# Feed-forward input by block products: four double groups instead of three, two of them with sums made by accumulating transfers

## The chip, the cores and the metric

One core of one Trainium2 chip runs the whole kernel. The metric is the device time of one execution in microseconds (us); smaller is better. Each measurement is a median over several runs.

## The reference

One layer of a hybrid decoder on 256 tokens of width 1024, in float32. Only the last part matters here, the gated feed-forward block with a hidden width of 2816:

```python
hn = rmsnorm(h, norm_ffn_g[l])
gu = hn @ w_ffn_in[l]                       # (256, 1024) @ (1024, 5632)
h = h + (jax.nn.silu(gu[..., :FFN_HIDDEN]) * gu[..., FFN_HIDDEN:]) @ w_ffn_out[l]
...
return rmsnorm(h, final_norm_g)
```

Before it come the attention, the recurrent branch, the merge and the cross-attention, which the change does not touch.

## The kernel before

**Precision.** Every float32 operand of a matmul is split into a high and a low part. ScalarE (ACT) copies the operand into a rounded type (`hi`), VectorE (DVE) subtracts to get `lo`, and TensorE (PE) multiplies three times: hi by hi, hi by lo, lo by hi. For a weight tile of 128x2048 this is `halve` (lines 1098 and 1099): one ACT copy and one DVE subtraction per tile.

**Groups and units.** The hidden width is cut into 11 groups of 256. A group has an input part in two units `("I", j, kh)`, one for each half of the 1024 features, and an output unit `("O", j)`. A unit is one weight tile of 1 MB. A direct input unit does 24 matmuls of 512 columns: two token halves, four feature blocks, three products. An output unit has 24 too, and adds into four accumulators (`acc`) that live to the end.

**Seven products for eight.** A double group (two neighbouring groups, q and q + 1) has four weight blocks: two feature halves by two groups. With two token halves that is a 2x2 by 2x2 product of blocks. Done directly it takes four units, 96 matmuls. `ffn_product` does it in Strassen's way with seven block products P1, P2, P6, P7, P5, P3, P4 of 12 matmuls, 84 in all. The price is sums and differences of blocks before the products (`block` and `load_blocks`, through `both`, line 1106: two DVE instructions of 1024 columns for each sum), sums of tokens made once (`token_sums`), and sums of results (`keep` on ACT and `whole` on DVE, line 1280, tile `fc`). Each product also needs a halving of its weight block, so a double group needs seven halvings where four units need four.

**Gate and transposes.** `gate` (lines 1205 and 1208) applies the silu on ACT (`fg`) and multiplies on DVE (`fu`). When both token halves of a group are gated, `turn_hid` transposes the result on PE (`hidT`, line 1215) and `split` makes its two parts (`hids`, lines 310 and 311). The output unit of that group reads them.

**Order.** PE's order is written out by hand: `FFN_PLAN` lists the units, `TURNS` says ahead of which unit a group's transposes come, and `LOADS` ahead of which unit the four blocks of a double group are loaded. The orders of ACT, DVE, GpSimd (POOL) and of the DMA issues on SyncE (SP) are set by a planner when the kernel is built: it takes an instruction when its inputs and buffers are free by its own estimates, earlier program text first. On the chip each queue then runs in that fixed order. Before, the units are: groups 0 and 1 direct, the double group 2 and 3, group 4 direct, double group 5 and 6, group 7 direct, double group 8 and 9, group 10 direct, with output units in between.

**Buffers.** Halved tiles rotate through four places (three pairs `hi`/`lo` and one pair `px` for every fourth unit), so halving runs at most four units ahead of PE. Raw tiles for direct and output units have two buffers. The four blocks of a double group have one buffer each (`b` in the profile, tags B10, B11, B12, B6), so the next double group's loads wait until the last reads of the present one. Four banks of the accumulation memory (`mm`) serve the products A, B and F and the transposes.

**The block before the first unit.** The norm of the second token half goes through a small power on POOL (`r`, line 1164), then a scaling on ACT (`hn`), PE transposes (`h2T`) and DVE, before the second direct matmuls and the token sums.

Of the kernel before, what the change touches and what calls it, by code (L numbers as in the profile page):

```python
# [97 lines left out]
def lay(ws):  # L98
# [45 lines left out]
def build(tc, A, out):  # L144
    nc = tc.nc
    V, SC, G, PE, SY = nc.vector, nc.scalar, nc.gpsimd, nc.tensor, nc.sync
    with ExitStack() as ctx:
# [940 lines left out]
        def halve(raw, n):  # L1088
            if n % 4 == 3:
                hi, lo = px[:, 0:2048], px[:, 2048:4096]  # L1090
            else:
                hi = wh.tile([128, 2048], F32R, name="hi", tag="hi")
                lo = wl.tile([128, 2048], F32R, name="lo", tag="lo")
            pieces = 2 if n < 2 else 1
            w = 2048 // pieces
            for c in range(pieces):
                a = slice(c * w, (c + 1) * w)
                SC.activation(hi[:, a], raw[:, a], AF.Copy)  # L1098
                V.tensor_tensor(lo[:, a], raw[:, a], hi[:, a].bitcast(F32), op=ALU.subtract)  # L1099
            return hi, lo  # L1100

# [5 lines left out]

        def load_blocks(q):
            blk.clear()
            for key, tag, c in (("22", "B12", (q + 1, 1)), ("12", "B6", (q + 1, 0)),  # L1110
                                ("11", "B10", (q, 0)), ("21", "B11", (q, 1))):
                blk[key] = big(tag, "b" + key, (128, 2048))
                SY.dma_start(blk[key], A["w"][where[("I",) + c]])
# [5 lines left out]
        def less(out, x, c):  # L1119
            SC.activation(out, x, AF.Copy, scale=-1.0)  # L1120
            G.dma_start(out, A["w"][where[("I",) + c]], accum_op=ALU.add)

        def block(q, name):
            if name == "P7" and BY_DMA:
                less(blk["21"], blk["11"], (q, 1))
# [73 lines left out]
        X2 = (h2h, h2l)  # L1199
        hid, acc, psi, hm = {}, {}, {}, {}  # L1200

        def gate(o, t):
            ps = psi.pop((o, t))
            g = t2b("fg", (128, 256))
            SC.activation(g, ps[:, 0:256], AF.Silu)
            if o not in hm:
                hm[o] = t2("fu", (128, 2, 256))
            V.tensor_tensor(hm[o][:, t], ps[:, 256:512], g, op=ALU.mult)

        def turn_hid(o):  # L1210
            bk = mm.tile([128, 2, 256], F32, name="hidT", tag="mm")
# [29 lines left out]
        def token_sums():  # L1241
            a11, a12, a21, a22 = (h2g[t, c] for t in range(2) for c in range(2))

            def put(i, g):
                SC.activation(SS[:, 0, i], g, AF.Copy)
                V.tensor_tensor(SS[:, 1, i], g, SS[:, 0, i].bitcast(F32), op=ALU.subtract)

            V.tensor_tensor(a22, a21, a22, op=ALU.add)
            s2 = t2("s2", (128, 4, 128))
            V.tensor_tensor(s2, a22, a11, op=ALU.subtract)  # L1250
# [4 lines left out]
            V.tensor_tensor(a12, a12, s2, op=ALU.subtract)  # L1255
            put(3, a12)

        def tokens(name):
# [18 lines left out]

        def whole(q, t, ps, key):
            c = t2("fc")
            V.tensor_tensor(c, ps, kept.pop(key), op=ALU.add)  # L1280
            psi[q, t] = c
            gate(q, t)

        def ffn_product(n):
# [8 lines left out]
            if name == "P1":  # L1293
                keep("1", ps, t2("f1"))
            elif name == "P2":
                whole(q, 0, ps, "1")
            elif name == "P6":
                keep("2", ps, gf[:, 1024:1536])
            elif name == "P5":
                keep("4", ps, gf[:, 1536:2048])  # L1300
                whole(q + 1, 1, bank_of["F"], "4")
            elif name == "P3":
                psi[q + 1, 0] = ps
                gate(q + 1, 0)
            elif name == "P4":
                whole(q, 1, ps, "2")
# [149 lines left out]
```

## Time and profile before

| | |
|---|---|
| median of three runs | 620.22 us (620.06 to 620.54) |
| the profiled execution's own time | 619.96 us |
| its span | 618.2 us |
| PE busy | 607.5 us, 98% |
| DVE busy | 460.0 us, 74% |
| ACT busy | 355.2 us, 57% |
| POOL busy | 256.5 us, 41% |
| DMA, share of 16 engines | 46.5% for the main queue, 107.50 MB |

Times in the rows are microseconds from the start of the span, unless ns is written. PE is the matrix engine, PEld its loading of weights, which overlaps. A row such as `lo<-raw,hi` names the tile written and the tiles read; L1099 is line 1099 of the kernel. The wait lists name the engine and instruction that waited, the one it waited for, the total, the number of times and the longest. The chain of waits is followed back from the last instruction, at each step to what released it. SPq rows are issues of transfers; their length is the time to issue. The feed-forward stage runs from about 430 us to 610 us of the span.

### The profile page before, as it was taken

The numbers are of one execution on the slowest core, as the hardware profiler recorded it, in microseconds if no ns is written. First come the engines' busy times: TensorE is split into PE (matmuls) and PEld (weight loads), VectorE is DVE, ScalarE is ACT, GpSimd is POOL, SyncE is SP. The second block draws the span as 40 slices with busy tenths as digits, with TensorE's granted clock in tenths as the row PEclk, the third lists the DMA queues.
The fourth block names the chain that finished last, engine by engine and source line by source line (L and its number), as shares of the span: only waits on it lengthen the run. The fifth ranks groups of instructions, "written<-read, shape, count | busy, mean of one in ns | idle before, by whom it ended". The sixth has DMA issues, their size and how long they took to land.

```text
span 618.2 us, 8376 instructions
## 1 busy us (share of the span) xinstructions
PE 607.5 (98%) x3117; PEld 506.7 (82%) x3117; DVE 460.0 (74%) x714; ACT 355.2 (57%) x545; POOL 256.5 (41%) x227
## 2 busy tenths in 40 slices
PE   8999999999999999999999999999998999999995
PEld 7888888888877877778888888888886888888884
DVE  7589988979766875747855456655799897997743
ACT  7785554334376756736456566746567556565432
POOL 3888744556544464355876876720000000000003
PEclk9999999999999999999999999999999999999999
DMA  8753553334543333644454554463815718613311
GB/s 346 289 204 150 205 200 140 137 136 140 189 150 136 137 137 124 208 181 149 191 205 152 193 200 156 163 227 142 335 68 193 283 69 325 218 68 137 141 64 68
DMA packets 16888, 107.50 MB, mean 174 GB/s; under 512 B 2000, under 2 KB 2640, under 8 KB 4560
## 3 DMA queue, kind: packets, MB, share of 16 engines
q1 hardware_dynamic: 16128, 106.14, 46.5%
q10 hardware_dynamic: 720, 0.84, 0.4%
q8 instruction: 24, 0.39, 0.2%
q14 instruction: 16, 0.13, 0.1%
HBM read 105.92 MB, written 1.05 MB: 173 GB/s over the span
## 4 chain that ended last, share of the span: by engine, by line
PE 89%; DVE 7%; issue 1%; ACT 1%; DMA 1%; POOL 0%; POOLq 0%; DVEq 0%; ACTq 0%
PE pst L263 13%; PE pst L265 13%; PE pst L264 13%; PE psf L284 7%; PE pqA L1269 4%; PE psf L285 4%; PE acc L265 3%; PE acc L263 3%; PE acc L264 3%; DVE lo L1099 2%; PE psi L263 2%; PE psi L265 2%; PE pqF L1269 2%; PE psi L264 2%; PE lp L638 2%; DVE b L1106 1%
## 5 line engine op out<-in xcount | busy, mean ns | idle before, releaser
L223 POOL TENSOR_TENSOR lo<-raw,hi 128x448 fp32r<-128x448 f32 x106 | 161.7, 1540 | 110.6 <-ACT hi L219 107.8
L219 ACT ACTIVATE hi<-raw 128x1024 fp32r<-128x1024 f32 (+1 forms) x128 | 128.7, 1028 | 93.7 <-PE pst L265 58.1
L223 DVE TENSOR_TENSOR lo<-raw,hi 128x576 fp32r<-128x576 f32 (+2 forms) x128 | 131.1, 1031 | 57.2 <-ACT hi L219 54.2
L263 PE MATMUL pst<-hi,XX 128*128 128x512 f32 x224 | 90.5, 404 | 0.0
L265 PE MATMUL pst<-hi,XX 128*128 128x512 f32 x224 | 87.4, 390 | 0.0
L264 PE MATMUL pst<-lo,XX 128*128 128x512 f32 x224 | 87.4, 390 | 0.0
L1374 POOL TENSOR_TENSOR hg<-H,gf 128x512 f32<-128x512 f32 x3 | 3.8, 1290 | 172.1 <-DVE H L1366 172.1
L1099 DVE TENSOR_TENSOR lo<-raw,hi 128x2048 fp32r<-128x2048 f32 (+1 forms) x21 | 43.7, 2086 | 12.2 <-ACT hi L1098 12.1
L265 PEld LDWEIGHTS pst<-hi,XX 128*128 128x128 f32 x224 | 42.1, 188 | 9.0
L263 PEld LDWEIGHTS pst<-hi,XX 128*128 128x128 f32 x224 | 42.1, 188 | 8.8 <-issue 0.7
L264 PEld LDWEIGHTS pst<-lo,XX 128*128 128x128 f32 x224 | 42.2, 188 | 7.8
L1098 ACT ACTIVATE hi<-raw 128x2048 fp32r<-128x2048 f32 (+1 forms) x21 | 36.6, 1750 | 16.4 <-issue 5.6
L1099 DVE TENSOR_TENSOR lo<-b,hi 128x2048 fp32r<-128x2048 f32 x13 | 29.8, 2289 | 8.0 <-ACT hi L1098 8.0
L265 PE MATMUL acc<-hi,hids 128*128 128x512 f32 x78 | 30.7, 393 | 1.7 <-DVE hids L311 1.7
L1098 ACT ACTIVATE hi<-b 128x2048 fp32r<-128x2048 f32 x13 | 24.9, 1914 | 12.1 <-PE acc L265 6.2
L263 PE MATMUL acc<-hi,hids 128*128 128x512 f32 x78 | 30.7, 393 | 0.0
L264 PE MATMUL acc<-lo,hids 128*128 128x512 f32 x78 | 30.4, 390 | 0.0
L1106 DVE TENSOR_TENSOR b<-b,b 128x1024 f32<-128x1024 f32 x24 | 28.5, 1219 | 0.0
L263 PE MATMUL psi<-hi,H 128*128 128x512 f32 x72 | 28.1, 391 | 0.0
L265 PE MATMUL psi<-hi,H 128*128 128x512 f32 x72 | 28.1, 390 | 0.0
L264 PE MATMUL psi<-lo,H 128*128 128x512 f32 x72 | 28.0, 389 | 0.0
L284 PE MATMUL psf<-H,hi 128*128 128x512 f32 x64 | 22.8, 400 | 0.0
(402 smaller groups left out, 1485.1 us busy)
## 6 DMA issues: line engine op xcount, KB each, us to landing
raw<-w SPq DMA_DIRECT2D x82, 1024.0 KB, 4.8
b<-w SPq DMA_DIRECT2D x12, 1024.0 KB, 5.9
raw<-w SPq DMA_DIRECT2D x4, 512.0 KB, 6.3
raw<-w SPq DMA_DIRECT2D x4, 256.0 KB, 4.0
H<-xtok SPq DMA_DIRECT2D x1, 1024.0 KB, 9.5
mraw<-mT SPq DMA_DIRECT2D x1, 1024.0 KB, 4.8
xraw<-xT SPq DMA_DIRECT2D x1, 512.0 KB, 6.4
gf<-gfin SPq DMA_DIRECT2D x1, 512.0 KB, 3.6
```

Source lines behind the costliest of these rows:

```text
L219: SC.activation(hi[:, a], raw[:, a], AF.Copy)
L223: eng.tensor_tensor(lo[:, b], raw[:, b], hi[:, b].bitcast(F32), op=ALU.subtract)
L263: PE.matmul(ps, xh, h, start=first, stop=False)
L264: PE.matmul(ps, xh, l, start=False, stop=False)
L265: PE.matmul(ps, xl, h, start=False, stop=last)
L284: PE.matmul(ps, w[0][:, k, a], X2[:, :, k], start=k == 0, stop=False)
L285: PE.matmul(ps[:, 0], w[1][:, k, a], X2[:, 0, k], start=False, stop=k == 7)
L638: PE.matmul(ps[:, j], KS[:, a0 + j], QQ[:, a0 + j], start=True, stop=True)
L1098: SC.activation(hi[:, a], raw[:, a], AF.Copy)
L1099: V.tensor_tensor(lo[:, a], raw[:, a], hi[:, a].bitcast(F32), op=ALU.subtract)
L1106: V.tensor_tensor(out[:, a], x[:, a], y[:, a], op=op)
L1269: PE.matmul(ps, x[k], z[:, k], start=first and k == 0 and i == 0, stop=k == 3 and i == 2, skip_group_check=not first)
```

## The change

A fourth double group replaces two direct groups. Direct are now groups 0, 1 and 6; double are 2 and 3, 4 and 5, 7 and 8, 9 and 10. The first two double groups follow each other, and so do the last two. `LOADS` and `TURNS` are set for the new order, and group 9's transposes stand in the middle of output unit 8 (`MIDWAY`).

In the double groups 2 and 7 (`BY_DMA`) two of the four block sums are made by transfers that POOL issues, which add into their destination: block 12 gets its second summand from memory in HBM (a further read of 1 MB), and block 21 has block 11 added to it from on-chip memory. The other two double groups make all four sums on DVE.

For a transfer that can only add, the two groups of a pair change places in the formulas and some blocks become sums where they were differences; the signs move to the token sums and, for P3 and P5, to the gate and to `whole`, which use the DVE form with two operators. `halve` copies `hi` in two pieces of 1024 columns for every unit.

```diff
-    out = two(0) + two(1)
-    out += seven(2, P2=[0], P5=[1]) + two(4)
-    out += seven(5, P2=[2], P7=[3], P5=[4]) + two(7)
-    out += seven(8, P2=[5], P7=[6], P5=[7])
-    out += two(10) + [("O", 8)]
+    out = two(0) + two(1) + seven(2, P7=[0], P5=[1])
+    out += seven(4, P7=[2], P5=[3]) + two(6)
+    out += seven(7, P7=[4], P5=[5])
+    out += seven(9, P7=[6], P5=[7], P4=[8])
     return out + [("O", 9), ("O", 10)]
...
-BY_DMA = False
-LOADS = {0: (2,), 10: (5,), 22: (8,)}
-TURNS = {4: (0,), 8: (1,), 15: (2,), 18: (3,), 20: (4,), 27: (5,), 30: (6,), 32: (7,), 38: (8, 9)}
+BY_DMA = (2, 7)
+LOADS = {0: (2,), 10: (4,), 19: (7,), 30: (9,)}
+TURNS = {4: (0,), 6: (1,), 13: (2,), 15: (3,), 24: (4,), 26: (5,), 33: (6,), 35: (7,), 38: (8,)}
+MIDWAY = {42: (9,)}
...
+            for c in range(2):
+                a = slice(c * 1024, (c + 1) * 1024)
+                SC.activation(hi[:, a], raw[:, a], AF.Copy)
...
-            for key, tag, c in (("22", "B12", (q + 1, 1)), ("12", "B6", (q + 1, 0)),
-                                ("11", "B10", (q, 0)), ("21", "B11", (q, 1))):
+            for key, tag, c in (("22", "B12", (q, 1)), ("12", "B6", (q, 0)),
+                                ("11", "B10", (q + 1, 0)), ("21", "B11", (q + 1, 1))):
...
-            if BY_DMA:
-                less(blk["12"], blk["12"], (q + 1, 1))
+            if q in BY_DMA:
+                G.dma_start(blk["12"], A["w"][where["I", q, 1]], accum_op=ALU.add)
             else:
-                both(blk["12"], blk["22"], blk["12"], ALU.subtract)
+                both(blk["12"], blk["22"], blk["12"], ALU.add)
...
             if name == "P6":
                 both(blk["11"], blk["12"], blk["11"], ALU.add)
+            elif name == "P7" and q in BY_DMA:
+                G.dma_start(blk["21"], blk["11"], accum_op=ALU.add)
             elif name == "P5":
-                both(blk["12"], blk["22"], blk["11"], ALU.subtract)
-            elif name == "P4" and not BY_DMA:
-                both(blk["21"], blk["21"], blk["11"], ALU.subtract)
+                both(blk["12"], blk["11"], blk["22"], ALU.subtract)
+            elif name == "P4" and q not in BY_DMA:
+                both(blk["21"], blk["21"], blk["11"], ALU.add)
...
+            if sign < 0:
+                V.scalar_tensor_tensor(hm[o][:, t], ps[:, 256:512], sign, g, op0=ALU.mult, op1=ALU.mult)
...
                     out_part(units[n][1], w, t, c)
+                if t == 0:
+                    for o in MIDWAY.get(n, ()):
+                        turn_hid(o)
```

The rest of the diff exchanges q and q + 1 in `ffn_product`, moves the signs in `token_sums` and `whole`, and removes `less`.

More of the change, by code (lines that the diff above doesn't have):

```diff
@@ L1200, in build, with gate @@
         hid, acc, psi, hm = {}, {}, {}, {}
-        def gate(o, t):
+        def gate(o, t, sign=1.0):
             ps = psi.pop((o, t))
             g = t2b("fg", (128, 256))
-            SC.activation(g, ps[:, 0:256], AF.Silu)
+            SC.activation(g, ps[:, 0:256], AF.Silu, scale=sign)
             if o not in hm:
                 hm[o] = t2("fu", (128, 2, 256))
-            V.tensor_tensor(hm[o][:, t], ps[:, 256:512], g, op=ALU.mult)
+            if sign < 0:
+                V.scalar_tensor_tensor(hm[o][:, t], ps[:, 256:512], sign, g, op0=ALU.mult, op1=ALU.mult)
+            else:
+                V.tensor_tensor(hm[o][:, t], ps[:, 256:512], g, op=ALU.mult)
         def turn_hid(o):
@@ L1279, in whole @@
             c = t2("fc")
-            V.tensor_tensor(c, ps, kept.pop(key), op=ALU.add)
+            if key == "4":
+                V.scalar_tensor_tensor(c, ps, -1.0, kept.pop(key), op0=ALU.mult, op1=ALU.subtract)
+            else:
+                V.tensor_tensor(c, ps, kept.pop(key), op=ALU.add)
             psi[q, t] = c
@@ L1295, in ffn_product @@
             elif name == "P2":
-                whole(q, 0, ps, "1")
+                whole(q + 1, 0, ps, "1")
             elif name == "P6":
@@ L1300, in ffn_product @@
                 keep("4", ps, gf[:, 1536:2048])
-                whole(q + 1, 1, bank_of["F"], "4")
+                whole(q, 1, bank_of["F"], "4")
             elif name == "P3":
-                psi[q + 1, 0] = ps
-                gate(q + 1, 0)
+                psi[q, 0] = ps
+                gate(q, 0, -1.0)
             elif name == "P4":
-                whole(q, 1, ps, "2")
+                whole(q + 1, 1, ps, "2")
         def ffn_out(n):
```

12 lines of the change are left out of this document (3 added, 9 removed).

## The prediction

> **What bounds the kernel now.** The page's line of engines comes first, then a table of windows over the feed-forward stage. The stage is cut at 430.47 (first matmul of `ffn_in`), 482.00 (first group of seven and its two output units done), 538.50 and 588.30 (the other two groups), and 610.17 (last output matmul). Columns: window and its length, then busy time of PE, PEld, DVE, ACT and POOL with the number of instructions, granted clock, DMA share, GB/s.
>
> ```profile
> PE 607.5 (98%) x3117; PEld 506.7 (82%) x3117; DVE 460.0 (74%) x714; ACT 355.2 (57%) x545; POOL 256.5 (41%) x227
> 430.47:482.00 51.53, 49.16 (x222) 39.84 (x221) 46.75 (x45) 31.73 (x33) 0.56 (x1) 1.00 0.55 220
> 482.00:538.50 56.50, 56.50 (x257) 46.80 (x256) 50.42 (x40) 34.45 (x29) 0.00 (x0) 1.00 0.59 224
> 538.50:588.30 49.80, 49.80 (x228) 41.19 (x227) 39.08 (x31) 27.48 (x24) 0.00 (x0) 1.00 0.31 113
> 588.30:610.17 21.87, 21.87 (x105) 18.23 (x104) 9.34 (x11) 6.21 (x11) 3.04 (x3) 1.00 0.08 32
> ```
>
> PE is the bound: from 482.00 on it is never idle. Only the first window has idle PE time, 51.53 - 49.16 = 2.37 us. What ends it stands in the list of waits and in the chain (start, length, what):
>
> ```profile
> PEld acc L265 <- DVE hids L311: 2.5, 2, 2.1
> PE acc L265 <- DVE hids L311: 1.7, 1, 1.7
> PE pqA L1269 <- ACT gf L1275: 0.7, 1, 0.7
> 473.90 2.20 DVE px L1099
> 476.11 0.61 DVE hids L311
> 482.06 2.72 PE pqA L1269 x12
> 484.78 2.72 PE pqF L1269 x12
> ```
>
> Before 476 the chain runs through DVE, where the split of hidden group 1 (`hids`) sat behind halvings of weights; afterwards it is PE. So the stage has two near-limits: PE nearly everywhere, DVE where a group of seven is worked off (46.75 of 51.53, 50.42 of 56.50).
>
> **The prices.** From the chain, one product (12 matmuls) takes 2.72 us of PE; a direct unit has 24 such matmuls, 5.44. DVE prices are pitches in its timeline, start to start:
>
> ```profile
> 459.54 2.28 DVE L1099 TENSOR_TENSOR lo<-b,hi 128x2048 fp32r<-128x2048 f32 x1
> 461.74 2.29 DVE L1099 TENSOR_TENSOR px<-b,px 128x2048 fp32r<-128x2048 f32 x1
> 463.94 0.69 DVE L1280 TENSOR_TENSOR fc<-pqB,f 128x512 f32<-128x512 f32 x1
> 464.54 1.22 DVE L1106 TENSOR_TENSOR b<-b,b 128x1024 f32<-128x1024 f32 x1
> 465.67 0.42 DVE L1208 TENSOR_TENSOR fu<-fc,fg 128x256 f32<-128x256 f32 x1
> 466.00 3.50 DVE L1106 TENSOR_TENSOR b<-b,b 128x1024 f32<-128x1024 f32 x3
> 613.66 0.88 DVE L1410 SCALAR_TENSOR_TENSOR H<-H,r_f,gf 128x256 f32<-128x256 f32 x2 [0.66 <-POOL r_f L1377]
> L1098 ACT ACTIVATE hi<-b 128x2048 fp32r<-128x2048 f32 x13 | 24.9, 1914 | 12.1 <-PE acc L265 6.2 <-DVE b L1106 4.7 <-ACT px L1098 0.6
> ```
>
> A halving costs 2.20 us (461.74 - 459.54), a 512-wide step 0.60, half a block sum 1.13 (a whole one 2.27), a gate 0.33. The last two rows are for later: two-operator steps of 256 columns, 0.44 each, and the ACT copy of a halving, 1.91.
>
> **The change part by part.** *Fourth group of seven.* Four direct units (96 matmuls) become seven products (84): PE gains 12 matmuls, **-2.72 us**. It lies on the path wherever PE is the bound. ACT and DVE get three more halvings (6.6 us of DVE), three `fc` (1.8) and, on ACT, three keeps; ACT has 51.53 - 31.73 = 19.8 us free in the tightest window, so they cost nothing there.
>
> *Two sums by transfers.* Block sums on DVE were 3 x 4 = 12 and are 2 x 4 + 2 x 2 = 12; the new group brings four and the transfers take four. In the first group DVE loses two, 4.5 us. That is more than the 2.37 us of idle PE there, and the output unit 1, whose `hids` PE waited for, has less DVE work in front of it: **-2.37 us**. At worst the stall stays (0).
>
> *Direct groups that stood between the sevens.* They gave DVE room: a direct group needs 2 x 2.20 + 2 x 0.33 = 5.1 us of DVE under 10.9 of PE. In the new order two sevens come back to back, twice. One pair with its four output units needs on DVE 18 halvings (39.6), 6 sums (13.6), 6 `fc` and 4 `hids` (6.0) and 8 gates (2.6), together 61.8 us, and on PE 14 x 2.72 + 4 x (5.44 + 0.44 of transposes) = 61.6 (0.44 is half of the chain's row of eight transposes below). DVE has no room in a pair at all; what hides its work is the lead with which it enters, and a queue that is served a little out of turn shows on PE. The nearest row is PE's one long wait on DVE, 1.7 us for `hids`; per pair I bound it by 0 (a wait cannot be less) and 1.7 and take half: **+1.7 us** for both pairs.
>
> *Transposes moved up.* Group 2's transposes stood behind two direct units; now they follow P4 at once, so P3's gate is covered by P4's 2.72 us alone. How late that gate is, the DVE timeline tells; P3 is the `pqA` row at 482.06, and P4 the `pqF` row, ending at 487.50. For the third group:
>
> ```profile
> 577.44 2.72 PE pqA L1269 x12
> 580.16 2.72 PE pqF L1269 x12
> 488.58 0.42 DVE L1208 TENSOR_TENSOR fu<-pqA,fg 128x256 f32<-128x256 f32 x1
> 493.91 0.42 DVE L1208 TENSOR_TENSOR fu<-fc,fg 128x256 f32<-128x256 f32 x1
> 581.69 0.42 DVE L1208 TENSOR_TENSOR fu<-pqA,fg 128x256 f32<-128x256 f32 x1
> 588.33 0.87 PE hidT L1215 x8
> 591.04 1.28 DVE L311 TENSOR_TENSOR hids<-hidT,hids 128x512 fp32r<-128x512 f32 x2
> ```
>
> In the first group the gate ended at 489.00, 1.5 us after P4; in the third at 582.11, before P4's end at 582.88. So 0 to 1.5; the first group's row is nearest, since DVE is full there: **+1.5 us**. Group 3's gate ended 494.33 - 487.50 = 6.8 us after P4; its cover is now the wait of 1.5, 0.44 of transposes and two products, 7.4: 0 (to 1).
>
> *Group 9's transposes in the middle of output unit 8.* Their split must be done when the second half of that unit ends, 2.72 us later. The nearest row is the split that ended at 592.32, 3.1 us after its transposes (589.20): **+0.4 us** (0 to 1.2, if one halving of 2.20 stands ahead).
>
> *Signs and split copies.* The token sums keep their number of DVE instructions, in the two-operator form, as does the gate; `hi` becomes two copies of 1024. The two-operator row lasts 0.44 against 0.42 for the one-operator gate of the same width, so 0; the split lets ACT begin while the second half of a sum is made, worth up to 1 us of latency where P6, P5 or P4 is late, taken as 0.
>
> *Loads and queues.* The new blocks' loads go out in the order in which the four buffers come free, as now:
>
> ```profile
> 425.94 0.33 SPq L1145 DMA_DIRECT2D raw<-w  x1
> 427.95 4.00 SPq L1113 DMA_DIRECT2D b<-w  x4
> 469.56 2.49 SPq L1113 DMA_DIRECT2D b<-w  x2
> 476.13 3.13 SPq L1113 DMA_DIRECT2D b<-w  x2
> DMA to landing us min/median/max: 4.8/5.9/10.1
> 428.00:430.00 2.00, 2.00 (x10) 1.67 (x9) 2.00 (x2) 0.37 (x1) 0.00 (x0) 1.00 0.97 410
> 442.00:444.00 2.00, 2.00 (x10) 1.67 (x9) 1.98 (x4) 0.38 (x1) 0.00 (x0) 1.00 1.08 446
> 438.64 1.03 PE L1177 MATMUL h2T<-cst,hn 128*128 128x128 f32 x8
> 453.49 0.48 PE L1269 MATMUL pqA<-hi,H 128*128 128x512 f32 x1
> 473.72 1.91 ACT L1098 ACTIVATE hi<-b 128x2048 fp32r<-128x2048 f32 x1
> 435.12 0.56 POOL L1164 TENSOR_TENSOR r<-v,nhalf 128x1 f32<-128x1 f32 x1 [13.93 <-DVE v L1162]
> 607.00 2.57 POOL L1374 TENSOR_TENSOR hg<-H,gf 128x512 f32<-128x512 f32 x2 [171.33 <-DVE H L1366]
> ```
>
> The last block of a second group, free about 479, lands at 479.3 + 5.9 = 485.2 and is halved (1.91 and 2.20) by 489.3. PE would ask for it, as P2, at 487.50 - 2.37 + 0.44 + 1.5 + 2.72 = 489.8. That is only just covered; late by 1 us it costs 1 us, and no more work hides it. POOL has nothing between 435.7 and 607, so the four accumulating transfers queue behind one small power and in front of nothing, if the planner leaves that power (`r`, on the way to PE's transposes at 438.64) ahead of them; behind the first transfer, which waits for block 12 until about 436, it would cost 1 to 2 us.
>
> *The accumulating transfer's own time, T.* No row shows one. The first can start when block 12 has landed: one raw load and two blocks at 1.05 MB per 2.45 us (the windows' 410 to 446 GB/s) plus landing, about 436. P6's sum must start on DVE by 454 (P1 starts on PE at 453.49, so P6 is due at 453.49 + 2 x 2.72 + 0.44 = 459.4; 2.20 for `lo`, half of 1.91 for the second half copy and 2.27 for the sum go off). So T up to 18 us is hidden. The nearest rows are loads of the same 1 MB, 4.8 to 10.1 us; a sum also reads where it writes, so twice that, 9.6 to 20.2, bounds it from above. I take 10, near twice the shortest, so 0; the upper end is a rival. The Trainium skill ("Collectives: The Full Stack", The bandwidth ceiling) says that a transfer that adds reads two sources and so moves twice the source traffic, the adding itself costing nothing; worked out from that, an estimate of 7.3 us for T, and the same sum. No run shown here has such a transfer.
>
> **Sum.** -2.72 - 2.37 + 1.7 + 1.5 + 0.4 = -1.5 us. The profiled execution's own time is 619.96 us (span 618.2 and 1.8 around it), so 618.5; the median of the three runs is 0.26 higher, so **618.7 us**.
>
> **The rivals.** *The gain is waited away.* If the pairs cost 1.7 each, the first group's stall stays by half (1.2) and the last block comes 1 us late, the sum becomes -1.5 + 1.7 + 1.2 + 1.0 = +2.4: 622.6; halfway there from the forecast is 620.7. For it speaks that 61.8 us of DVE stand against 61.6 of PE in both pairs; against it that in the window from 538.50, with a group of seven and a direct one, DVE was idle for 10.7 us, and that PE waited for nothing for 128 us on end. Its middle is no change, its outer half slower.
>
> *The accumulating transfer is late* (the other side). Place: P6 of units 2 and 3, where the sum of blocks 11 and 12 needs the transfer, and then P4, which needs the second one: that starts after P6's sum, about 454, and P4's copy started at 473.7 now, so it has about 19.5 us. Price: T - 18 there and T - 19.5 here. It decides from T = 19.5, where the 1.5 us are used up; at T = 22 it costs 4 + 2.5, giving 618.7 + 6.5 = 625.2. For it: the queue is full (share 0.97 to 1.08) from 428 to 444, just when the first transfer starts, and 20.2 is the end of the bound. Against it: twice the shortest row is 9.6. The Trainium skill ("DMA: Bandwidth & Descriptors", Issuing engines are not separate DMA queues) says that transfers from all queues interleave on the same 16 engines; the trace's full share agrees that there is no room beside them, and by that rule the first T would grow by its own length, which is why this rival has more than a small chance.
>
> *All covers hold.* Pairs and transposes cost nothing: 620.22 - 5.1 = 615.1.
>
> **How the numbers follow.** A measurement of this kernel can tell about 0.2%, 1.24 us, from no change: faster is below 618.98, slower above 621.46. Forecast and the case with all covers: 0.47 (all covers 0.07 of it). Gain waited away: 0.33, of which 0.16 lands within the bound and 0.17 above. Late transfer: 0.20, all slower. So faster 0.47, same 0.16, slower 0.37. The range leaves out most of the all-covers case below, and of the late transfer what lies beyond T = 21.7: 616.3 to 624.5. The forecast's own range is 616.3 to 619.0.
>
> **What would show it.** Right: the chain stays on PE; idle PE up to the end of output unit 1 falls from 2.37 to under 0.5; short PE waits on `fu` before group 2's transposes (about 1.5) and on DVE's halvings in the second and fourth groups (together about 1.7); the matmul count falls by 12; the POOL queue's transfers land within 18 us. Wrong: a PE wait ahead of P6 or P4 of the first or third group that ends with a transfer; PE waits of more than 3.5 us in sum on `lo`; transposes of `h2T` later than 439, because the power stands behind a transfer in POOL's queue.

## The result: 622.38 us, slower by 0.35%

The changed kernel takes 622.38 us (median of six runs, 622.23 to 622.99); the kernel before, measured on the same chip between them, takes 620.19 us (six runs, 620.06 to 620.63). The ratio is 1.0035, 95% interval 1.0023 to 1.0046. The forecast was 618.7 us and faster; the time lies in the forecast's range (616.3 to 624.5), on its other side.

The profiled execution took 622.99 us, 3.03 us more than that of before: 0.53 of it outside the span (2.29 against 1.76 us), the rest in the span (620.7 against 618.2). From the page of the changed kernel: engines, chain, two transfer queues (packets, MB, share of the 16 engines over the span; q0 holds the four adding transfers alone), and the adding transfers (count, KB each, median us from issue to landing).

```profile
PE 606.9 (98%) x3105; PEld 504.5 (81%) x3105; DVE 467.0 (75%) x720; ACT 366.2 (59%) x594; POOL 260.3 (42%) x231
...
PE 74%; DVE 11%; DMA 7%; issue 3%; ACT 3%; POOL 0%; POOLq 0%; DVEq 0%; SPq 0%; ACTq 0%
...
q1 hardware_dynamic: 16128, 106.14, 46.2%
q0 software_dynamic: 576, 4.19, 3.3%
...
b<-w POOLq DMA_DIRECT2D x2, 1024.0 KB, 12.4
b<-b POOLq DMA_DIRECT2D x2, 1024.0 KB, 7.0
```

The twelve matmuls are gone (3117 to 3105). But PE's busy time fell by 0.6 us only, and the chain that ends last now passes through DVE for 11% of the span and through transfers for 7%, where it had been 89% PE, 7% DVE and 1% transfers. The windows of the changed kernel say where. The first is cut at its first `ffn_in` (431.56) and ends with the first double group's products, the next ends at 519.90 with the second's, 519.90 to 531 is the direct group 6, then come the third and fourth double groups and the last output units. The last row is for the adding transfers: in that stretch nothing else was moving.

```profile
431.56:482.90 51.34, 51.05 (x233) 42.16 (x232) 42.63 (x41) 33.08 (x44) 2.55 (x3) 1.00 0.80 273
482.90:519.90 37.00, 34.13 (x152) 27.33 (x151) 35.39 (x27) 25.02 (x32) 0.88 (x1) 1.00 0.51 174
519.90:531.00 11.10, 11.10 (x51) 9.19 (x50) 8.29 (x8) 4.29 (x5) 0.00 (x0) 1.00 0.89 322
531.00:559.70 28.70, 28.24 (x129) 23.05 (x128) 25.84 (x21) 18.48 (x24) 0.90 (x1) 1.00 0.75 254
559.70:592.50 32.80, 31.63 (x146) 25.98 (x145) 31.54 (x26) 24.03 (x30) 0.00 (x0) 1.00 0.18 67
592.50:612.77 20.27, 19.41 (x91) 15.77 (x90) 10.12 (x12) 5.34 (x10) 3.06 (x3) 1.00 0.15 52
...
458.00:460.00 2.00, 2.00 (x11) 1.65 (x10) 2.00 (x2) 2.00 (x4) 0.00 (x0) 1.00 0.98 197
```

Idle PE time, window minus busy: 0.29, 2.87, 0, 0.46, 1.17 and 0.86, together 5.65 us, where it was 2.37 us before, all in the first group. The stage, cut at the same two places as in the prediction, takes 181.21 us against 179.70. So +1.51 us = 3.28 more idle less 1.77 of busy time. The list of PE's waits in the changed kernel gives the releasers:

```profile
PE pqA L1271 <- DVE lo L1101: 2.8, 3, 1.3
PE pqB L1271 <- DVE lo L1101: 1.4, 1, 1.4
PE acc L265 <- DVE hids L311: 0.9, 1, 0.9
PE pqB L1271 <- DVE fu L1210: 0.5, 1, 0.5
```

All six end with DVE; the other 0.10 us of idle time lies ahead of group 2's transposes. The rest of the profiled difference in the span is 1.09 us between the start and the stage (it begins at 431.56 against 430.47), which the change doesn't touch. The experiments below begin the stage anywhere from 430.56 to 431.18, with and without adding transfers, so I take this as scatter. (PE is busy 429.91 us before the stage, against 428.82, which is why the page shows only 0.6 us less of busy PE time in all, where the stage alone has 1.77 less.) By medians the difference is 2.19 us: 0.5 outside the span, and, if the profiled stage is typical, 1.5 in the stage; 0.2 stay unassigned.

The largest wait, at P2 of the second group, read through four engines' timelines (start, length, what, in brackets the idle time before it and what ended it):

```profile
476.15 2.53 SPq L1115 DMA_DIRECT2D b<-w  x2
...
485.60 2.01 ACT L1096 ACTIVATE hi<-b 128x1024 fp32r<-128x1024 f32 x2 [2.09 <-DMA b<-w]
...
483.17 2.36 DVE L1108 TENSOR_TENSOR b<-b,b 128x1024 f32<-128x1024 f32 x2 [1.71 <-DMA b<-w]
485.44 0.42 DVE L1208 SCALAR_TENSOR_TENSOR fu<-pqA,fg 128x256 f32<-128x256 f32 x1
485.78 2.35 DVE L1108 TENSOR_TENSOR b<-b,b 128x1024 f32<-128x1024 f32 x2
488.04 0.69 DVE L1285 TENSOR_TENSOR fc<-pqF,gf 128x512 f32<-128x512 f32 x1
488.64 2.28 DVE L1101 TENSOR_TENSOR lo<-b,hi 128x2048 fp32r<-128x2048 f32 x1
...
489.15 0.39 PE L1271 MATMUL pqB<-hi,H 128*128 128x512 f32 x1
490.98 0.50 PE L1271 MATMUL pqB<-lo,H 128*128 128x512 f32 x1 [1.44 <-DVE lo L1101]
491.31 0.63 PE L1271 MATMUL pqB<-hi,H 128*128 128x512 f32 x2
...
506.72 0.50 PE L1271 MATMUL pqA<-lo,SS 128*128 128x512 f32 x1 [1.33 <-DVE lo L1101]
...
525.05 1.23 DVE L1108 TENSOR_TENSOR b<-b,b 128x1024 f32<-128x1024 f32 x1 [1.39 <-DMA b<-w]
...
534.92 0.50 PE L1271 MATMUL pqB<-hi,H 128*128 128x512 f32 x1 [0.46 <-DVE fu L1210]
```

The first row holds two issues: block 22's at 476.15, and block 21's behind it, at about 478.4 (the row's end less the 0.33 of one issue), since block 21 of the second group could be fetched only when P4 of the first had been halved. It was there at 485.60, copied by ACT until 487.6; DVE made a block sum and an `fc` first and halved it from 488.64 to 490.84. PE had stood since 489.5. The last three rows are P5 of the same group, and, for later, a sum of the third group that waited for an adding transfer, and P2 of that group.

### The profile page after: what moved, and what is told of

It is laid out like the page before. It is cut to its first block, busy times and chain, and to the rows that moved or that the text cites. A ratio compares the mean times of both kernels' runs of the same rounds, so it can differ in the third digit from the quotient of the medians.

```text
span 620.7 us, 8432 instructions
## 1 busy us (share of the span) xinstructions
PE 606.9 (98%) x3105; PEld 504.5 (81%) x3105; DVE 467.0 (75%) x720; ACT 366.2 (59%) x594; POOL 260.3 (42%) x231
## 3 DMA queue, kind: packets, MB, share of 16 engines
q1 hardware_dynamic: 16128, 106.14, 46.2%
q0 software_dynamic: 576, 4.19, 3.3%
## 4 chain that ended last, share of the span: by engine, by line
PE 74%; DVE 11%; DMA 7%; issue 3%; ACT 3%; POOL 0%; POOLq 0%; DVEq 0%; SPq 0%; ACTq 0%
PE pst L263 13%; PE pst L265 12%; PE pst L264 12%; PE psf L284 7%; DMA b<-w 6%; DVE lo L1101 5%; PE psf L285 4%; PE pqA L1271 2%; ACT hi L1096 2%; DVE b L1108 2%; PE lp L638 2%; DVE px L1101 2%; DMA raw<-w 2%; PE psg L539 1%; PE pqF L1271 1%
## 5 line engine op out<-in xcount | busy, mean ns | idle before, releaser
L1096 ACT ACTIVATE hi<-b 128x1024 fp32r<-128x1024 f32 x44 | 44.3, 1051 | 21.8 <-DMA b<-w 8.9
L1101 DVE TENSOR_TENSOR lo<-b,hi 128x2048 fp32r<-128x2048 f32 x22 | 50.1, 2286 | 8.3 <-ACT hi L1096 8.3
L1101 DVE TENSOR_TENSOR lo<-raw,hi 128x2048 fp32r<-128x2048 f32 (+1 forms) x14 | 27.6, 1979 | 6.7 <-ACT hi L1096 6.7
L1117 POOL DMA_DIRECT2D b<-w x2 | 2.0, 996 | 61.7 <-DMA b<-w 55.1
L1096 ACT ACTIVATE hi<-raw 128x1024 fp32r<-128x1024 f32 x24 | 24.4, 1051 | 2.1 <-DMA raw<-w 2.1
L263 PE MATMUL acc<-hi,hids 128*128 128x512 f32 x62 | 24.2, 390 | 0.0
L265 PE MATMUL acc<-hi,hids 128*128 128x512 f32 x62 | 24.1, 389 | 0.0
L264 PE MATMUL acc<-lo,hids 128*128 128x512 f32 x62 | 24.1, 389 | 0.0
L284 PE MATMUL psf<-XX,hi 128*128 128x512 f32 x64 | 22.9, 401 | 0.0
L284 PE MATMUL psf<-M,hi 128*128 128x512 f32 x64 | 22.5, 396 | 0.0
## 6 DMA issues: line engine op xcount, KB each, us to landing
b<-w POOLq DMA_DIRECT2D x2, 1024.0 KB, 12.4
```

The costliest lines, as they stand in the source:

```text
L263: PE.matmul(ps, xh, h, start=first, stop=False)
L264: PE.matmul(ps, xh, l, start=False, stop=False)
L265: PE.matmul(ps, xl, h, start=False, stop=last)
L284: PE.matmul(ps, w[0][:, k, a], X2[:, :, k], start=k == 0, stop=False)
```

## The experiments

**1. Do the transfers help?** All sixteen sums on DVE, the rest as in the changed kernel.

```diff
-BY_DMA = (2, 7)
+BY_DMA = ()
```

> The changed kernel with all block sums on DVE again, no transfer that adds (BY_DMA empty). Theory A (queue order and fixed costs): the changed kernel loses 5.6 us of PE waits, most of them in the second and fourth groups, which make their sums on DVE in both versions, and about 0.5 us outside the span plus some at the start because transfers from POOL exist at all. Then here the time outside the span falls from 2.3 back to 1.8 us, the waits of the second and fourth groups stay at about 4 us, and the first group's wait of about 2 us comes back: 623 to 624.5. Rival B (DVE throughput): every sum given back to DVE costs its full 2.27 us, four of them: 629 or more. Rival C (the adding transfers get in the way of the blocks' loads): without them the waits on transfers go and the time falls below 621.

Measured: 625.28 us, ratio to before 1.0077 (1.0061 to 1.0093): slower than the changed kernel, so the transfers do relieve DVE. The time lies between what theory A (to 624.5) and rival B (from 629) had named. The wait ahead of output unit 1 in the first group did not come back, although DVE had its two sums again; but P6 of that group now waited 1.33 us, where it waits 0.28 in the changed kernel, so the first group had 1.33 us of idle PE time (first window below). And after one of two waits of about 2 us PE ran at half its clock. Timeline rows and windows of this kernel (granted clock third from the end):

```profile
491.61 0.50 PE L1271 MATMUL pqB<-lo,H 128*128 128x512 f32 x1 [2.13 <-DVE lo L1101]
...
568.58 0.50 PE L1271 MATMUL pqB<-lo,H 128*128 128x512 f32 x1 [2.01 <-DVE lo L1101]
```

```profile
431.00:483.00 52.00, 50.67 (x231) 41.57 (x230) 46.38 (x44) 33.03 (x44) 0.56 (x1) 1.00 0.55 221
...
493.00:495.00 2.00, 2.00 (x6) 1.52 (x6) 2.00 (x3) 2.00 (x4) 0.00 (x0) 0.50 0.00 0
...
560.00:593.00 33.00, 30.68 (x140) 24.78 (x140) 32.08 (x27) 23.66 (x30) 0.00 (x0) 1.00 0.22 85
```

**2. Does a POOL transfer cost something by itself?** The kernel before, with one transfer of 32 KB that POOL issues and nobody reads.

```diff
+        tiny = cp.tile([128, 64], F32, name="tiny")
...
+            if n == 10:
+                G.dma_start(tiny, A["w"][0][:, 0:64])
```

> The kernel before with one plain transfer of 32 KB issued from POOL in the middle of the feed-forward stage into a tile that nobody reads. If a program with any transfer from POOL pays a fixed cost (outside the span and at the start), the time rises by 0.5 to 1 us to 620.7 to 621.2, the time outside the span from 1.8 to 2.3 us, and the feed-forward stage is as before (179.7 us). Rival: the cost belongs to the four large transfers, or is chance of one execution: 620.2, and 1.8 us outside.

Measured: 620.50 against 620.44 us, ratio 1.0000 (0.9990 to 1.0009). No fixed cost shows: the time outside the span is 1.78 us in both, and the interval leaves room for 0.6 us at most.

**3. Are the sums in DVE's queue in the way of P2?** In the second and fourth groups the sums for P6 are ordered behind P2's halving.

```diff
-            if name == "P6":
+            if name == "P6" and q in BY_DMA:
                 both(blk["11"], blk["12"], blk["11"], ALU.add)
+            elif name == "P6":
+                with tc.issue_after(last[0]):
+                    both(blk["12"], blk["22"], blk["12"], ALU.add)
+                    both(blk["11"], blk["12"], blk["11"], ALU.add)
```

> The changed kernel, with the sums of blocks 12 and 11 of the second and fourth groups queued on DVE behind the halving of P2's block, instead of ahead of it. Theory A (queue order): DVE no longer stands 1.7 us for block 22 while P2's block is ready, PE's wait of 1.44 us ahead of P2 of the second group goes, and about as much is gained: 620.7 to 621.5. Rival B (DVE has no time in a pair whatever its order): the wait moves to P6 or P5 of the same group and the time stays at 622.4 within 0.4.

Measured: 632.32 us, ratio 1.0186 (1.0145 to 1.0227). The wait at P2 halved, but P6 paid for it, and P6's eleven matmuls behind that wait took 4.98 us, where a whole product takes 2.72: the granted clock was 0.50 from 497 to 503. PE's timeline of this kernel:

```profile
489.05 0.50 PE L1273 MATMUL pqB<-lo,H 128*128 128x512 f32 x1 [0.72 <-DVE lo L1101]
493.92 0.44 PE L1219 MATMUL hidT<-cst,fu 128*128 128x128 f32 x2 [1.87 <-DVE fu L1212]
498.32 4.98 PE L1273 MATMUL pqA<-px,SS 128*128 128x512 f32 x11 [3.71 <-DVE px L1101]
```

So this order does not help: DVE is busy almost without a break there (35.39 of 37.00 us in the changed kernel's window from 482.90), and the sums that it makes later are missed by P6. Whether another order would do better, runs 10 to 12 tell.

**4. The split copies.** `halve` with one ACT copy of 2048, as before.

> The changed kernel with the ACT copy of a halving in one piece of 2048 columns again. Theory A: in the changed kernel the pieces of two or three tiles stand interleaved on ACT (from 465.5 to 471.2 us six pieces of three tiles), which ends each tile later; in one piece, DVE's waits for ACT shrink and the time falls by 0.3 to 1.5 us to 621 to 622. Rival: the split lets ACT start on the first half of a sum, and without it P6, P5 and P4 come up to 1 us later each: 623 to 624.

Measured: 624.02 us, ratio 1.0057 (1.0042 to 1.0073). The waits at P5 of the second and fourth groups went, others came. From the list of waits of this kernel:

```profile
PE pqB L1269 <- DVE lo L1099: 1.9, 1, 1.9
PE pqB L1269 <- DVE fu L1208: 1.3, 1, 1.3
```

By the two ratios the split copies are worth about 1.4 us in the new order; the intervals just touch (1.0042 here, 1.0046 in the changed kernel).

**5 and 6. Is it block 22?** In the second and fourth groups block 22 goes to a raw tile instead of its single buffer, so its load need not wait for P3's halving; first with split copies, then with one copy.

```diff
+                if key == "22" and q in (4, 9):
+                    blk[key] = wr.tile([128, 2048], F32, name="raw", tag="raw")
+                else:
+                    blk[key] = big(tag, "b" + key, (128, 2048))
```

> The changed kernel with block 22 of the second and fourth groups in one of the two raw tiles instead of its own buffer, so that its load need not wait until P3 of the group before has been halved (476.1 us in the changed kernel's trace; it landed at 483.1 with DVE waiting 1.7 us for it). Theory A2 (the late buffer of block 22 starts the waits of the back-to-back pairs): DVE makes the sum of blocks 12 and 22 while PE still works on the group before, PE's waits ahead of P2 and P5 of the second group (1.44 and 1.33) go, and perhaps P5's of the fourth (1.17): 618.5 to 620.5. Rival B (a pair has 61.8 us of DVE work for 61.6 of PE, whenever its blocks arrive): the waits move to later products, 622.4 within 0.5.

> The early block 22 together with the copy in one piece. Theory A2 with the wait ahead of P5 due to interleaved pieces: this one is the fastest of the four-group kernels, 618 to 620, with no PE wait over 1 us and so no stretch of half clock. Rival: the split is needed where sums feed P6; then it is slower than the early block 22 alone by 0.5 to 1.5 us.

Measured: 628.15 us, ratio 1.0126 (1.0111 to 1.0141), and 626.94 us, 1.0108 (1.0093 to 1.0123). P2 of the second group still waited 1.34 us: not block 22. And the direct group 6, which needs both raw tiles, now starved, for 3.31 and then 2.48 us in PE's timeline of the first of the two:

```profile
528.33 0.79 PE L263 MATMUL psi<-px,H 128*128 128x512 f32 x1 [3.31 <-ACT px L1096]
```

**7 and 8. Signs, split copies and transfers in the old order.** The changed kernel with the unit list, loads and transposes of before; once with the first group's two sums by transfers, once with all on DVE.

```diff
-BY_DMA = (2, 7)
-LOADS = {0: (2,), 10: (4,), 19: (7,), 30: (9,)}
-TURNS = {4: (0,), 6: (1,), 13: (2,), ...}
+BY_DMA = (2,)
+LOADS = {0: (2,), 10: (5,), 22: (8,)}
+TURNS = {4: (0,), 8: (1,), 15: (2,), ...}
```

> Three double groups in the order of the kernel before (units, loads and transposes as before), with the new signs, the copies in two pieces and the two adding transfers in the first group alone. If the transfers free DVE in the first group as the changed kernel's trace shows (PE idle 0.3 us up to 483 instead of 2.4), and two of them cost about half of the 0.5 us outside the span: 618 to 619. Rival: the transfers take so much of the 16 engines (12.4 and 7.0 us to landing) that the blocks' loads come late and nothing is gained: 620.2 within 0.4.

> The same without any adding transfer: the kernel before with the new signs and the copies in two pieces. If these two are free, as the prediction had it: 619.8 to 620.6, with the first group's idle time of PE as before (about 2.4 us). Rival: the copies in two pieces stand interleaved and end the tiles later, 621 or more; or they let ACT start on half sums, and the idle time falls by about 1 us: 619.2.

Measured: 620.06 us, ratio 0.9999 (0.9990 to 1.0009), and 620.21 us, 1.0000 (0.9990 to 1.0010). In the old order signs and split copies are free, within the 0.6 us of the interval. With the transfers DVE did less in the first group (43.0 us of 51.4 against 46.7), and PE's longest wait stayed as it was (list of waits of the kernel with transfers; the lines are that kernel's):

```profile
PE acc L267 <- DVE hids L313: 1.8, 1, 1.8
```

PE's other wait in the first group, 0.64 us without the transfers, did go with them, and the profiled stage was about 1 us shorter; in the times this does not show clear of noise.

**9. What then removed that wait?** Two more things differ there: output unit 0 stands behind P7 instead of P2, and group 1's transposes come two tiles earlier. Here is the kernel before with the second of them alone.

```diff
-TURNS = {4: (0,), 8: (1,), 15: (2,), ...
+TURNS = {4: (0,), 6: (1,), 15: (2,), ...
```

> The kernel before with one thing of the change: the transposes of group 1's hidden units are placed at tile 6 instead of tile 8. Theory A (the idle time of 2.37 us that the kernel before had in its first group was a matter of order in the queues: the copies to hids stood behind a later halving, so that output unit 1 began late): that wait vanishes and nothing takes its place, 617.9 to 618.6, faster than the kernel before by 1.8 to 2.5. Rival B (DVE is short of time there, as the prediction had it): the wait moves to another product of the first group, 619.8 to 620.8. Rival C (the earlier transposes stand on PE before the hidden units are there): 0.3 to 1 us new wait at tile 6, 618.6 to 619.6.

Measured: 618.84 us against 620.60, ratio 0.9966 (0.9954 to 0.9978). Theory A holds for the long wait: `hids` is gone from PE's list of waits, so that wait was a matter of place in the queues, not of DVE's load. Not all idle time went with it: the wait for `gf`, 0.69 us before, is now 0.99, and one of 0.28 is new, so the first group keeps 1.27 of its 2.37 us. The time is 1.76 us shorter by medians.

```profile
PE pqA L1269 <- ACT gf L1275: 1.0, 1, 1.0
PE pqA L1269 <- DVE lo L1099: 0.3, 1, 0.3
```

**10. Is it block 21?** Output units 1 and 5 stand behind P4 instead of behind P5, so that P4 is halved, and block 21's buffer free, one output unit earlier than PE needs the next P2.

```diff
-    out = two(0) + two(1) + seven(2, P7=[0], P5=[1])
+    out = two(0) + two(1) + seven(2, P7=[0], P4=[1])
...
-    out += seven(7, P7=[4], P5=[5])
+    out += seven(7, P7=[4], P4=[5])
```

> The changed kernel with output units 1 and 5 placed behind the last product of their group (P4) instead of behind P5. What the tiles compute is unchanged. In the changed kernel block 21 of the second group could be loaded only once P4 of the first had been halved (load issued at 476.15, landed about 485.5), and PE asked for P2 of the second group 1.44 us before its halving was done (490.98). Theory A (the block's arrival after P4's halving is the start of that chain): P4 is now halved some 5.5 us earlier relative to PE's need of P2, because a unit of 5.4 us of matmul work stands between them; the waits at P2 of the 2nd and 4th groups go below 0.3 us and, as DVE is less late afterwards, the one at P5 (1.33 us) shrinks to below 0.7; time 619.0 to 621.0, faster than the changed kernel by 1.4 to 3.4. Rival B (DVE's load of sums, not the block, is what is late): the waits stay the same to within 0.5 us, 622 to 623. Rival C (the products P5, P3, P4 now follow each other without an output unit and a halving or the late sum of block 21 becomes late): a new wait of 1 to 3 us at P3 or P4 of the first group, 621.5 to 625.

Measured: 621.19 us, ratio 1.0010 (0.9998 to 1.0021); the interval lies below that of the changed kernel. Theory A's mechanism is shown for the second group, its time just missed. The profiled execution (623.16 us) is one of the longer of the twelve (620.05 to 623.40), so its waits are those of a long one. The timeline of this kernel: PE at P3 of the first group, then ACT and DVE for block 21 of the second group, PE at its P5, POOL, DVE and PE in the third, and PE at P5 of the fourth:

```profile
474.62 0.50 PE L1271 MATMUL pqA<-hi,SS 128*128 128x512 f32 x1 [0.69 <-ACT gf L1277]
...
482.02 2.01 ACT L1096 ACTIVATE hi<-b 128x1024 fp32r<-128x1024 f32 x2 [3.37 <-DMA b<-w]
...
484.72 2.28 DVE L1101 TENSOR_TENSOR lo<-b,hi 128x2048 fp32r<-128x2048 f32 x1
...
504.44 0.50 PE L1271 MATMUL pqA<-lo,SS 128*128 128x512 f32 x1 [0.15 <-DVE lo L1101]
...
511.50 0.88 POOL L1117 DMA_DIRECT2D b<-w  x1 [54.57 <-DMA b<-w]
...
524.45 1.23 DVE L1108 TENSOR_TENSOR b<-b,b 128x1024 f32<-128x1024 f32 x1 [3.04 <-DMA b<-w]
...
533.90 0.50 PE L1271 MATMUL pqB<-hi,H 128*128 128x512 f32 x1 [1.68 <-DVE fu L1210]
...
583.50 0.50 PE L1271 MATMUL pqA<-lo,SS 128*128 128x512 f32 x1 [1.29 <-DVE lo L1101]
```

The block was copied 3.6 us earlier than in the changed kernel (1.0 of it because the stage began earlier in this execution), halved by 486.9, and P2 did not wait; P5 after it waited 0.15 instead of 1.33. In place of these came 0.69 us twice at P3, which now stands right behind P5 and goes on in the bank that ACT copies out, and 1.68 us at P2 of the third group. That one begins with an adding transfer: issued at 511.50, it ended at about 524.45, and DVE stood idle 3.04 us for it. P5 of the fourth group waited as long as before (1.29 us, 1.17 in the changed kernel).

**11. Is the third group's adding transfer late?** As 10, with the third group's sums on DVE.

```diff
-BY_DMA = (2, 7)
+BY_DMA = (2,)
```

> The changed kernel with output units 1 and 5 behind P4, and with the third group's two sums on DVE instead of by adding transfers (the first group's two stay). Theory A (in the third group the adding transfer itself is what is late: it was issued at 511.50 and landed 12.4 us later, DVE stood idle 3.04 us for it at 524.45, and from that sum on the halving of P5 and the gate behind it were late, which was PE's wait of 1.68 us at P2's bank): with the sum on DVE, which has idle time at 521 to 524, that wait goes below 0.4 us and the time falls by 1 to 2 us against the kernel with both pairs of transfers, to 619.2 to 620.2. If the time outside the span goes with the number of adding transfers, it is 1.76 to 1.85 with two, instead of 2.06 to 2.4. Rival B (DVE is short there, and the transfers do relieve it): a wait of 1 to 3 us at P2, P6 or P5 of the third group in its place, 621 to 623.

Measured: 620.47 us, ratio 1.0000 (0.9991 to 1.0010), a little above theory A's range, and against run 10 not clear of noise (the intervals overlap). The mechanism is shown: its list of PE waits has no `fu` any more, and the 1.29 us at P5 of the fourth group are gone too:

```profile
PE pqA L1271 <- ACT gf L1277: 1.4, 2, 0.7
PE acc L265 <- DVE hids L311: 0.8, 1, 0.8
PE pqF L1271 <- DVE fc L1283: 0.7, 2, 0.4
PE pqA L1271 <- DVE lo L1101: 0.3, 2, 0.2
```

The time outside the span fell from 2.06 us to 1.79.

**12. And the two waits at P3?** As 11, with output units 0 and 4 behind P5.

```diff
-    out = two(0) + two(1) + seven(2, P7=[0], P4=[1])
+    out = two(0) + two(1) + seven(2, P5=[0], P4=[1])
...
-    out += seven(7, P7=[4], P4=[5])
+    out += seven(7, P5=[4], P4=[5])
```

> As the last one, but output units 0 and 4 stand behind P5 instead of behind P7, so that P3, which goes on in P5's bank, no longer stands right behind it. Theory A: PE's two waits of 0.69 us for the copy of P5's bank (ACT to gf) go, and nothing takes their place: 618.0 to 619.6. Rival B: P7 and P5 now follow each other with no output unit between them, and P5's sum, which writes the block that P7 reads, has 5.5 us less; PE waits 1 to 2.5 us at P5 of the first and third group: 620.5 to 623.

Measured: 618.92 us against 620.34, ratio 0.9981 (0.9971 to 0.9990), in theory A's range and below run 11, though not quite by its mechanism: the waits at P3 went, and 1.01 us came at P5 of the first group, which now waits for ACT's copy of P6's bank, and 0.55 at P6 of the second and fourth. Its list of PE waits, then two windows, cut at 482, 520 and 560 us (columns as above):

```profile
PE pqA L1271 <- DVE px L1101: 1.1, 2, 0.6
PE pqA L1271 <- ACT gf L1277: 1.0, 1, 1.0
...
482.00:520.00 38.00, 37.29 (x168) 30.33 (x167) 36.39 (x30) 24.93 (x31) 0.00 (x0) 1.00 0.51 192
520.00:560.00 40.00, 40.00 (x182) 33.11 (x181) 39.67 (x32) 25.61 (x33) 0.00 (x0) 1.00 0.49 193
```

In the second window DVE was busy for 39.67 of 40.00 us, more than in the changed kernel (34.34 in the same stretch), and PE never waited. So DVE's load alone does not make PE wait; what it has in front of it when PE asks does.

Versions 9 and 12 both beat both kernels; their intervals touch, so which of the two is faster stays open. Version 12 has the early transposes too, so nothing here shows that the fourth double group by itself brings any time.

## Why the prediction was wrong, step by step

**Fourth group, -2.72.** Right in the count. On the path it brought less: busy PE time in the stage fell by 1.77 us. What is missing lies around the waits. In the timeline above, the three starts 489.15, 490.98 and 491.31 span 2.16 us: two matmuls at their usual 0.227 are 0.45, the wait in brackets is 1.44, and 0.27 remain, which the brackets leave out: the row before the wait lasts 0.39 and the next start after it comes 0.33 later. (The profile models the ends of matmuls, so how the 2.16 splits is its choice; the starts are not.) The six waits of the changed kernel have 0.27 to 0.37 of this each, 1.8 together; the two of before had 0.5, and before lost another 0.3 without any idle time, where three starts (459.27, 459.68, 460.01) span 0.74 us. That makes -2.72 + 1.8 - 0.8 = -1.7. I counted waits by their brackets alone.

**Two sums by transfers, -2.37.** The size came (idle time in the first group fell from 2.37 to 0.29), but for the larger part the reason was wrong, and that it fits is luck. Runs 7, 1 and 9 show it for the long wait, 1.67 us for `hids`: transfers in the old order left it standing, the new order without transfers was free of it, and moving the transposes alone removed it. The transfers did their part for the rest: without them the first group had 1.33 us of idle time in the new order (run 1), and in the old order they took away the wait of 0.6 to 0.7 (run 7). The chain before had shown it: `hids` came right behind a halving, at 476.11. I read that row as DVE being late by load, when DVE only had another instruction first.

**Pairs back to back, +1.7, and transposes moved up, +1.5.** This is the failing step. Together 3.2 were taken and idle PE time of 2.87 + 0.46 + 1.17 = 4.5 us was measured, of which only 0.10 stands at group 2's transposes. So the pairs cost 4.4, not 1.7, above even the bound of 3.4. The bound took the longest single wait of the trace for a whole pair; but in this order several products of a pair come without lead, and each can wait. The sign that the prediction had named for this, more than 3.5 us of PE waits on `lo` in sum, came: 2.8 and 1.4. The prediction gave the equal work of DVE and PE (61.8 against 61.6) as the reason. Run 12 says that this is not enough: with two sums more on DVE in the second pair, and another order, the waits in the second and fourth groups came to 1.25 us, and those in the third to nothing.

The prediction had also worked out the largest wait and let it go at 0. Block 21 was to land at 485.2 and be halved by 489.3, and PE to ask at 489.8. PE asked at 489.5 and the block was copied from 485.60, which looks nearly right, but the stage had begun 1.09 us later than in the trace of before. Counted from the stage's first matmul, P2 was to start at 59.3 and did at 57.6 (489.15 - 431.56); its halving was to be done at 58.8 and was at 59.3 (490.84 - 431.56). So PE came 1.7 us earlier than worked out: the 1.5 us for group 2's transposes had been counted as a cost and, in the same sum, as cover for this block, and they did not come. And DVE came 0.5 us later, although the block was there sooner: the 2.20 us for the halving assumed that DVE would take it at once, but it had a block sum and an `fc` first. Runs 3 and 10 show both halves: sums moved out of the way were missed by P6, and an earlier block removed the wait.

**Group 9's transposes, +0.4.** 0.86 measured, within its bounds of 0 to 1.2.

**Signs and split copies, 0.** Right in the old order (run 8). In the new order the split copies were worth about 1.4 us (run 4), where the prediction had named up to 1 us and taken 0.

**T of the adding transfer: 10, hidden.** It took 12.4 us from HBM and 7.0 on chip. In the first group it was hidden but for a remainder: DVE waited 0.39 us for it ahead of P6's sum, and PE 0.28 at P6. In the third it was not: DVE waited 1.39 us for it in the changed kernel and PE 0.46 behind that, and in run 10 1.68; run 11, with these sums on DVE, is free of both. The prediction allowed 18 us, worked out for the first group; the third's was never worked out. The small power `r` stood ahead of the transfers on POOL (433.97 against 441.10), so the sign of transposes of `h2T` later than 439 came only by the letter: they began at 439.73, but 8.17 us after the stage's first matmul, exactly as before. The rival "transfer late" thus named the right kind of wait, at the wrong group and far too dear.

**Outside the span, 0.** 2.25 us (2.22 to 2.30, six runs) against 1.78. The prediction had no term for this; it is described at the end.

The sum with measured sizes: -2.72 + 1.0 for the waits' edges - 2.08 for the first group + 4.5 for pairs and transposes + 0.86 + 0.5 = +2.1 us, where the medians say +2.2. Against the forecast's -1.5 that is 3.6 us more: 1.3 from pairs and transposes, 1.0 from the edges, 0.5 from group 9's transposes, 0.5 from outside the span and 0.3 from the first group. The pairs and transposes are the largest item; without it the sum would still be +0.8. Of the rivals, "the gain is waited away" (622.6) came nearest, by its pairs and its late block. That its number fits is in part luck: its third part, a first stall that stays by half, did not happen, and the edges and the time outside the span, which it did not have, took that place.

## What to carry to other kernels

When a wait is removed by a change that does two things at that place, undo them one by one before believing either: here moving one group's transposes by two tiles was worth 1.76 of the 2.37 us that the transfers were credited with. Where an engine's work equals the bound's over a stretch, count a wait for each single-buffered step in it, not one for the stretch, add about 0.3 us for each wait's edges (by these traces), and work out each cover with the helper's queue in front of it, not with the helper free. A wait that is counted as a cost in one place must not be counted on as cover in another. Look first for a place in the order that gives the buffer back sooner: in run 10 that removed the largest wait, at the price of others, and run 12, with a further change of order and two adding transfers fewer, has about 2.4 us of idle PE time in the stage where the changed kernel has 5.65.

## What the runs showed of the hardware

**An adding transfer moves about half as fast.** On the page of the changed kernel the four adding transfers (q0) took 3.3% of the engines' time for 4.19 MB. Over the span of 620.7 us that is 20.5 us, or about 205 GB/s at a full share; the main queue's 106.14 MB in 46.2% give about 370. The window in which an adding transfer was alone shows 197 GB/s at a share of 0.98, where plain loads had 410 to 446 at such shares in the prediction's rows. The Trainium skill ("Collectives: The Full Stack", The bandwidth ceiling) says of the reducing step of a collective that its add needs two source reads and so reaches half the rate of a copy; the trace agrees. The estimate of 7.3 us for T stands beside 7.0 on chip and 12.4 from HBM.

**The clock halved after some waits of about 2 us, not after all.** Behind the 2.13 us in run 1, the granted clock was 0.50 from 493 to 495, and behind a wait of 1.87 us in run 4 it was 0.54 in the same stretch. But the 2.01 us at 568.58 in run 1 left it at 1.00 (window from 560 to 593), as did one of 1.88 us in run 6, and waits of 1.44 us and less in the changed kernel. What decides between them no run here shows. The Trainium skill ("TensorE: Matmul & The Clock Gate", What's actually happening) says that the halved clock comes after at least one idle window of about 3.4 us; here shorter waits were enough, so the trace differs from the page by that. Where it happens, a wait near 2 us is dearer than its length: the eleven matmuls of P2 from that wait to the next transposes took 4.07 us in run 1 (491.61 to 495.68), against 2.65 in the changed kernel (490.98 to 493.63).

**Four adding transfers go with more time outside the span.** Every kernel with four had 2.06 to 2.38 us there (medians of the changed kernel and of runs 3, 4, 5, 6 and 10); every kernel with two or fewer 1.76 to 1.83, run 11 among them, which differs from run 10 only in making two sums on DVE instead of by transfers. What happens in that time no trace shows; it stays open.
